# A gate product moved ahead of a head's q and k in the filling work of a decoder block on one Trainium2 core

## The chip, the core and the metric

The kernel runs on one core of one Trainium2 chip. The metric is the device time of one execution in microseconds. The engines are TensorE (PE, with its weight loads as PEld), VectorE (DVE), ScalarE (ACT), GpSimd (POOL) and SyncE (SP, which issues the loads). PSUM is the memory that PE writes its products to.

## The reference

One layer of a decoder block for 512 tokens of width 1024: an input projection, two causal attention branches (MLA with 8 heads, differential attention with 4 heads), a gated merge, an output projection and a SwiGLU network of width 2816.

```python
xn = rmsnorm(x, norm_mix_g[l])
proj = jnp.einsum('bsd,de->bse', xn, w_in[l])
q_lat, kv_lat, k_rope, dq, dk, dv, gate_pre = jnp.split(proj, split_idx, axis=-1)
...
o_mla = causal_attention(q_mla, k_mla, v_mla).reshape(B, S, MLA_WIDTH)
...
o1 = causal_attention(dq[..., 0, :], dk[..., 0, :], dv)
o2 = causal_attention(dq[..., 1, :], dk[..., 1, :], dv)
o_diff = rmsnorm(o1 - lam * o2, diff_subln_g[l]) * (1.0 - lambda_init)
...
gates = jax.nn.sigmoid(gate_pre + b_gate[l])
g_mla, g_diff = gates[..., :D_MODEL], gates[..., D_MODEL:]
merged = (g_mla * jnp.einsum('bse,ed->bsd', o_mla, w_branch_mla[l])
          + g_diff * jnp.einsum('bse,ed->bsd', o_diff, w_branch_diff[l]))
x = x + jnp.einsum('bsd,de->bse', merged, w_out[l])
hn = rmsnorm(x, norm_ffn_g[l])
hid = jax.nn.silu(jnp.einsum('bsd,df->bsf', hn, w_ffn_gate[l])) * jnp.einsum('bsd,df->bsf', hn, w_ffn_up[l])
x = x + jnp.einsum('bsf,fd->bsd', hid, w_ffn_down[l])
```

## The kernel before

Every product of full precision is made of three matmuls (`mm3`, L299 to L301): operands are split into a rounded high part and the remainder, and high times high, high times low and low times high are added up in PSUM. Weights come in tiles of 128 x 1024 (`weights`): SP loads them into `raw` (four buffers), ACT rounds them (L261) and DVE takes the difference (L266) into `w` (three buffers).

The attention of a head is a chain. Four blocks of scores (L627) of 128, 256, 384 and 512 columns go through a maximum on DVE (L631), an exponential on ACT (L159), a reciprocal (L634) and scaling (L681 and L680 for a differential head); PE transposes them (L653), ACT and DVE split the transposes into `PT` (L246, L250), and PE multiplies with V (L664, or L774 in MLA). For a differential head a norm follows in `diff_norm`: PE sums the squares with two matmuls against `ones_r` (L699) and ACT takes a logarithm and an exponential (L159).

This chain leaves PE idle, so it is filled with products that the attention doesn't wait for at once. Tables of "filling items" say which product is written into which stage: `FILL_MLA` for four pairs of MLA heads, `FILL_DIFF` for four differential heads. `("qk", h)` makes q and k of head h (two products of 24 matmuls, each read by the rotary on DVE with a shuffle, L558, and a multiplication, L559, and finished on POOL, L560 and L561). `("v", c)` makes V of heads 2c and 2c + 1: two PSUM tiles of 48 matmuls of 256 columns, scaled into SBUF by ACT (L248) and DVE (L252). `("gate", b, m)` makes one tile of gate pre-activations (24 matmuls), read by one DVE multiplication (L481). A scheduler orders all instructions on each engine ahead of time; attention has the higher priority (`urgent`), filling items take what is left, in the order in which they are written. Each engine then works its list in that order.

All these products write PSUM tiles called `ps_mm`, of which there are three buffers, taken in turn: a product starts only when the product three before it has been read.

Behind the last head, ACT loads another table and makes 16 sigmoids in place (`sigmoids`, L488), held behind the last exponential. The 16 products of the branches (`branch`, 12 matmuls each, also in `ps_mm`) are each multiplied with a gate by DVE (L792), which needs the sigmoid. The first of them need only the MLA result and begin while the last head's norm is still under way. The output projection and the SwiGLU network follow.

Of the kernel before, what the change touches and what calls it, by code (L numbers as in the profile page):

```python
# [47 lines left out]
            [("mqk", 2), ("mr", 2), ("gate", 0, 3), ("gate", 0, 4), ("mv", 1)],  # L48
            [("mqk", 3), ("mr", 3), ("qk", 0)],
            [("qk", 1)]]  # L50
FILL_DIFF = [[("qk", 2), ("v", 1)],
             [("qk", 3), ("gate", 0, 5), ("gate", 0, 6)],
             [("gate", 0, 7), ("gate", 1, 0), ("gate", 1, 1)],
             [("gate", 1, m) for m in range(2, KD)]]
PBUFS = dict(mm=3, sc=2, tr=2, pv=1)
# [33 lines left out]
def build(ctx, nc, tc, a, out):  # L89
# [51 lines left out]
    def urgent():  # L141
        return attention
# [351 lines left out]
    def fill(work):  # L494
        for kind, *args in work:
            if kind == "gate":
                gate(*args)
            elif kind == "v":
                diff_v(*args)
            elif kind == "qk":  # L500
                qk[args[0]] = diff_qk(*args)
            elif kind == "pe":
                pe[args[0]] = mla_pe(*args)
            elif kind == "mv":
                mv[args[0]] = mla_v(*args)
            elif kind == "mqk":
                mqk[args[0]] = mla_qk(*args)
            elif kind == "mr":
                mla_rope(args[0], mqk[args[0]], pe[args[0] // 2])
# [301 lines left out]
    for h in range(4):  # L811
        parts_first[0] = True
        fill(FILL_DIFF[h])
        with urgent():
# [185 lines left out]
```

## Time and profile before

| | |
|---|---|
| median of 3 runs | 740.13 us (740.10 to 741.04) |
| profiled execution | 740.23 us, span 738.5 us |
| busy PE, DVE, ACT, POOL | 729.0, 413.6, 333.7, 48.4 us |
| MLA attention ends, differential attention goes on | about 180 us |
| last differential head's PV products end, branch products start | 276 us, 280 us |

Busy time is how long an engine had an instruction under way; matmuls overlap, so their pace is read from one start to the next. Timeline rows give the start, the duration, engine, line, operation, output and inputs, shape and number of merged instructions, and in brackets the idle time before and who ended it.

### The profile page before, as it was taken

Reading aid. Unit: us, or ns where it says so; the run is one execution under the profiler, and the core shown is the slowest. Engines: PE = TensorE matmul, PEld = TensorE weight load, DVE = VectorE, ACT = ScalarE, POOL = GpSimd, SP = SyncE. Lnnn points to the kernel's source line nnn. Section 1 sums busy time; section 2 is a strip of 40 time slices with the busy share of each in tenths; the row PEclk is TensorE's granted clock in tenths of the full one; section 3 lists DMA queues with packets and bytes.
Section 4 is the critical chain, followed back from the end, with each engine's and each line's share of the span. In section 5 each row is a group of like instructions: output and inputs, shape, how many; then the busy total and the mean of one; then the engine's idle time right before and its main releaser. Section 6 shows DMA issues by size and latency. Waiting matters only on the chain.

```text
span 738.5 us, 9543 instructions
## 1 busy us (share of the span) xinstructions
PE 729.0 (99%) x3602; PEld 617.2 (84%) x3602; DVE 413.6 (56%) x812; ACT 333.7 (45%) x613; POOL 48.4 (7%) x45
## 2 busy tenths in 40 slices
PE   9999999999999999999999999999999999999996
PEld 7978988888888888888898888888888888888885
DVE  7789789988898765793634333333233232222514
ACT  7765678676766526561433223223232231212314
POOL 1000000322041101000000000000000000000303
PEclk9999999999999999999999999999999999999999
DMA  9615455323433312346204233332333323223203
GB/s 335 196 59 138 120 129 137 93 59 85 115 86 86 114 59 87 114 161 210 84 3 143 86 108 92 90 110 86 105 94 88 112 86 102 98 88 113 86 1 114
DMA packets 100414, 78.82 MB, mean 107 GB/s; under 512 B 6416, under 2 KB 87056, under 8 KB 100368
## 3 DMA queue, kind: packets, MB, share of 16 engines
q1 hardware_dynamic: 100080, 78.13, 35.9%
q8 instruction: 28, 0.46, 0.3%
q14 instruction: 18, 0.15, 0.1%
q10 hardware_dynamic: 288, 0.08, 0.0%
HBM read 71.91 MB, written 2.10 MB: 100 GB/s over the span
## 4 chain that ended last, share of the span: by engine, by line
PE 96%; DVE 3%; ACT 0%; issue 0%; DVEq 0%
PE ps_mm L299 25%; PE ps_mm L300 25%; PE ps_mm L301 25%; PE ps_sc L627 3%; PE ps_tr L653 2%; PE ps_tr L301 2%; PE ps_sc L300 2%; PE ps_sc L299 2%; PE ps_sc L301 2%; PE ps_tr L299 2%; PE ps_tr L300 2%; PE ps_pv L774 1%; PE ps_pv L664 1%; PE ps_pv L301 1%; PE ps_pv L300 1%; PE ps_pv L299 1%
## 5 line engine op out<-in xcount | busy, mean ns | idle before, releaser
L261 ACT ACTIVATE w<-raw 128x1024 fp32r<-128x1024 f32 (+3 forms) x110 | 109.4, 998 | 253.5 <-issue 150.7
L266 DVE TENSOR_TENSOR w<-raw,w 128x1024 fp32r<-128x1024 f32 (+3 forms) x114 | 133.7, 1175 | 159.8 <-ACT w L261 159.5
L299 PE MATMUL ps_mm<-X,w 128*128 128x512 f32 (+1 forms) x568 | 217.3, 383 | 0.1
L300 PE MATMUL ps_mm<-X,w 128*128 128x512 f32 (+1 forms) x568 | 216.8, 382 | 0.0
L301 PE MATMUL ps_mm<-X,w 128*128 128x512 f32 (+1 forms) x568 | 216.4, 381 | 0.0
L299 PEld LDWEIGHTS ps_mm<-X,w 128*128 128x128 f32 x568 | 106.7, 188 | 20.4 <-issue 0.3
L300 PEld LDWEIGHTS ps_mm<-X,w 128*128 128x128 f32 x568 | 106.9, 188 | 20.0 <-issue 0.2
L301 PEld LDWEIGHTS ps_mm<-X,w 128*128 128x128 f32 x568 | 106.8, 188 | 20.0
L905 DVE TENSOR_TENSOR t<-t,ps_mm 128x512 f32<-128x512 f32 x22 | 15.1, 688 | 66.8 <-PE ps_mm L301 66.1
L159 ACT ACTIVATE P<-P,sm 128x128 f32<-128x128 f32 (+3 forms) x64 | 35.7, 558 | 21.4 <-DVE sm L631 21.0
L931 POOL TENSOR_TENSOR L<-L,P 128x512 f32<-128x512 f32 (+1 forms) x9 | 12.6, 1421 | 434.8 <-ACT t L930 434.8
L627 PE MATMUL ps_sc<-L,L 96*128 96x128 f32 (+7 forms) x160 | 37.3, 327 | 0.2 <-DVE sm L631 0.2
L300 PE MATMUL ps_mm<-w,L 128*128 128x512 f32 (+1 forms) x100 | 37.3, 373 | 0.0
L299 PE MATMUL ps_mm<-w,L 128*128 128x512 f32 (+1 forms) x100 | 37.1, 373 | 0.0
L301 PE MATMUL ps_mm<-w,L 128*128 128x512 f32 (+1 forms) x100 | 37.0, 373 | 0.0
L300 PE MATMUL ps_mm<-L,w 128*128 128x512 f32 x90 | 35.4, 394 | 0.0
L299 PE MATMUL ps_mm<-L,w 128*128 128x512 f32 x90 | 35.4, 395 | 0.0
L301 PE MATMUL ps_mm<-L,w 128*128 128x512 f32 x90 | 35.1, 390 | 0.0
L631 DVE CUSTOM_DVE_ANT_0 P<-ps_sc,mask 128x128 f32<-128x128 f32 (+3 forms) x64 | 30.5, 477 | 5.8 <-PE ps_sc L627 5.0
L246 ACT ACTIVATE L<-t 64x512 fp32r<-64x512 f32 (+2 forms) x47 | 29.2, 621 | 6.9 <-PE ps_pv L301 3.7
L627 PEld LDWEIGHTS ps_sc<-L,L 96*128 96x128 f32 (+1 forms) x160 | 26.7, 189 | 3.3 <-DVE sm L631 0.4
L250 DVE TENSOR_TENSOR L<-t,L 128x512 fp32r<-128x512 f32 (+2 forms) x37 | 26.3, 711 | 3.5 <-ACT L L246 3.1
(271 smaller groups left out, 1136.8 us busy)
## 6 DMA issues: line engine op xcount, KB each, us to landing
raw<-w_in SPq DMA_DIRECT2D x28, 512.0 KB, 4.0
raw<-w_ffn_gate SPq DMA_DIRECT2D x22, 512.0 KB, 3.9
raw<-w_ffn_up SPq DMA_DIRECT2D x22, 512.0 KB, 3.9
raw<-w_ffn_down SPq DMA_DIRECT2D x22, 512.0 KB, 3.6
L<-x SPq DMA_DIRECT2D x8, 512.0 KB, 7.3
L<-L SPq DMA_DIRECT2D x32, 128.0 KB, 3.7
raw<-w_out SPq DMA_DIRECT2D x8, 512.0 KB, 3.9
L<-xt SPq DMA_DIRECT2D x8, 256.0 KB, 4.4
```

The costliest lines, as they stand in the source:

```text
L159: return nc.scalar.activation(**kw)
L246: nc.scalar.activation(out=hi, in_=src, func=AF.Copy, scale=scale)
L250: nc.vector.tensor_sub(out=lo, in0=src, in1=r32(hi))
L261: nc.scalar.activation(out=o, in_=i, func=AF.Copy)
L266: (nc.vector if w_eng[1] == 'dve' else nc.gpsimd).tensor_sub(out=o, in0=i, in1=r32(hi))
L299: nc.tensor.matmul(out=o, lhsT=lh, rhs=rh, start=start, stop=False)
L300: nc.tensor.matmul(out=o, lhsT=lh, rhs=rl, start=False, stop=False)
L301: return nc.tensor.matmul(out=o, lhsT=ll, rhs=rh, start=False, stop=stop)
L627: nc.tensor.matmul(out=ps[:, :n], lhsT=q[:, i * P:n], rhs=k[:, 0:n], start=j == 0, stop=j == last)
L631: nc.vector.tensor_tensor_reduce(out=m, in0=ps[:, :n], in1=mask[:, S - n:], scale=-1.0, scalar=3.4e38, op0=ALU.add, op1=ALU.min, accum_out ...
L653: nc.tensor.transpose(out=ps[:, c:c + P], in_=blocks[i][:, j * P:(j + 1) * P], identity=ident)
L905: nc.vector.tensor_mul(out=g, in0=g, in1=ps)
```

## The change

Gate product 5 of the first branch is written one stage earlier, ahead of q and k of the third differential head. The number of instructions of each kind stays the same.

```diff
-FILL_DIFF = [[("qk", 2), ("v", 1)],
-             [("qk", 3), ("gate", 0, 5), ("gate", 0, 6)],
+FILL_DIFF = [[("gate", 0, 5), ("qk", 2), ("v", 1)],
+             [("qk", 3), ("gate", 0, 6)],
```

The scheduler's lists differ from there to the first branch products. PE's list on V, near the end of the MLA attention, before: `ps_sc_2303` and `ps_sc_2304` are the fourth score block of differential head 0, `ps_mm_2179` is the second tile of V.

```order
L627 MATMUL ps_sc_2304<-L_1567,L_1566 128x512
L774 MATMUL ps_pv_2014<-PT_1994,L_1320 128x256
L774 MATMUL ps_pv_2014<-PT_1994,L_1320 128x128
L774 MATMUL ps_pv_2014<-PT_1994,L_1304 128x512
L774 MATMUL ps_pv_2014<-PT_1994,L_1304 128x384
L774 MATMUL ps_pv_2014<-PT_1994,L_1320 128x256
L774 MATMUL ps_pv_2014<-PT_1994,L_1320 128x128
L653 MATMUL ps_tr_2332<-ident,P_2233 128x128
L627 MATMUL ps_sc_2529<-L_1817,L_1815 128x128
L627 MATMUL ps_sc_2529<-L_1817,L_1816 128x128
L299 MATMUL ps_mm_2179<-w_2117,X_61 128x256
```

The same place after, from the fourth score block on: `ps_sc_2334` and `ps_sc_2335` are its two maps, `ps_mm_2156` the first tile of V.

```order
L627 MATMUL ps_sc_2334<-L_1567,L_1565 128x512
L627 MATMUL ps_sc_2334<-L_1567,L_1566 128x512
L301 MATMUL ps_mm_2156<-w_2153,X_62 128x256
L299 MATMUL ps_mm_2156<-w_2153,X_62 128x256
L300 MATMUL ps_mm_2156<-w_2153,X_62 128x256
L301 MATMUL ps_mm_2156<-w_2153,X_62 128x256
L627 MATMUL ps_sc_2335<-L_1567,L_1565 128x512
L627 MATMUL ps_sc_2335<-L_1567,L_1566 128x512
L653 MATMUL ps_tr_2356<-ident,P_2264 128x128
L774 MATMUL ps_pv_2014<-PT_1994,L_1320 128x256
```

Before, the first tile of V was done ahead of the fourth score block; now its last four matmuls stand between the two maps. Behind these rows come the other five PV matmuls, a transpose, two scores, two transposes and then V's second tile (`ps_mm_2210`).

DVE's list at the same place, before: `ps_mm_2033` is q of the third head.

```order
L634 RECIPROCAL sm_2294<-sm_2293 128x1
L631 ISA P_2301,sm_2309<-ps_sc_2303,mask 128x512
L631 ISA sm_2309 128x1
L679 TENSOR_TENSOR sm_2294<-sm_2294,neg_lam 128x1
L558 STREAM_SHUFFLE t_2059<-ps_mm_2033 128x512
L559 TENSOR_TENSOR t_2058<-ps_mm_2033,tab_595 128x512
```

And after, where q is `ps_mm_2064`:

```order
L631 ISA P_2332,sm_2340<-ps_sc_2334,mask 128x512
L631 ISA sm_2340 128x1
L681 SCALAR_TENSOR_TENSOR P_2309<-P_2309,sm_2319,P_2310 128x384
L634 RECIPROCAL sm_2342<-sm_2341 128x1
L558 STREAM_SHUFFLE t_2090<-ps_mm_2064 128x512
L559 TENSOR_TENSOR t_2089<-ps_mm_2064,tab_595 128x512
```

The reciprocal of this same score block (`sm_2341` is the sum that its exponential on ACT makes) now stands ahead of the rotary's reads of q.

PE's list behind the last differential head, before: `ps_tr_3229` is that head's norm, `ps_mm_3264` and `ps_mm_3278` are the first two branch products, and `ps_mm_3297` and `ps_mm_3311` the third and fourth.

```order
L299 MATMUL ps_mm_3278<-L_829,w_3261 128x512
L300 MATMUL ps_mm_3278<-L_829,w_3261 128x512
L699 MATMUL ps_tr_3229<-L_3226,ones_r 128x512
L301 MATMUL ps_mm_3278<-L_829,w_3261 128x512
L299 MATMUL ps_mm_3278<-L_1179,w_3261 128x512
```

After:

```order
L299 MATMUL ps_mm_3297<-L_1778,w_3294 128x512
L699 MATMUL ps_tr_3229<-L_3226,ones_r 128x512
L300 MATMUL ps_mm_3297<-L_1778,w_3294 128x512
L301 MATMUL ps_mm_3297<-L_1778,w_3294 128x512
L299 MATMUL ps_mm_3311<-L_829,w_3294 128x512
```

The second norm matmul stood three matmuls into the second branch product, with 22 of the second and third behind it; now it stands two matmuls ahead of the fourth one. The last head's PV products end 19 matmuls later in PE's list than before, the branch products follow directly, and the norm comes in among them.

## The prediction

> **What bounds the kernel now.** I read the busy times first, then who TensorE waits for, then its timeline at those places. The first two rows are from the page, the next three are all the waits of TensorE (PE) behind the first two microseconds (total, times, longest).
>
> ```profile
> span 738.5 us, 9543 instructions
> PE 729.0 (99%) x3602; PEld 617.2 (84%) x3602; DVE 413.6 (56%) x812; ACT 333.7 (45%) x613; POOL 48.4 (7%) x45
> ...
> PE ps_mm L299 <- DVE t L559: 0.9, 1, 0.9
> PE ps_pv L664 <- ACT PT L246: 0.2, 1, 0.2
> PE ps_sc L627 <- DVE sm L631: 0.2, 1, 0.2
> ```
>
> PE works 729.0 of 738.5 us. The change adds and removes no matmul, so the sum is about PE's waits alone. Two places hold all the waits shown. The first is the end of the MLA attention, where the second half of V starts (column two is the time of a row, matmuls overlap, so I count from start to start):
>
> ```profile
> 176.58 0.63 PE L627 MATMUL ps_sc<-L,L 128*128 128x512 f32 x2
> 177.05 0.57 PE L774 MATMUL ps_pv<-PT,L 128*128 128x512 f32 x2
> ...
> 178.53 1.08 PE L774 MATMUL ps_pv<-PT,L 128*128 128x256 f32 x6
> 179.45 0.28 PE L653 MATMUL ps_tr<-ident,P 128*128 128x128 f32 x1
> 179.91 0.44 PE L627 MATMUL ps_sc<-L,L 128*128 128x128 f32 x2 [0.18 <-DVE sm L631]
> 181.21 0.39 PE L299 MATMUL ps_mm<-w,X 128*128 128x256 f32 x1 [0.86 <-DVE t L559]
> 181.43 0.28 PE L300 MATMUL ps_mm<-w,X 128*128 128x256 f32 x1
> 181.55 0.28 PE L301 MATMUL ps_mm<-w,X 128*128 128x256 f32 x1
> ...
> 186.11 0.34 PE L627 MATMUL ps_sc<-L,L 128*128 128x128 f32 x2
> 186.29 0.33 PE L300 MATMUL ps_mm<-w,X 128*128 128x256 f32 x1
> ```
>
> A 256-wide matmul takes 0.12 us from start to start (181.43 to 181.55), two small scores 0.18 (186.11 to 186.29), a transpose about 0.11. Unhindered, the matmul at 181.43 would start at 179.45 + 0.11 + 0.18 + 0.12 = 179.86. Place A loses 1.57 us. The wait ends with the rotary reads (L558, L559) that free q's PSUM buffer. The second place, at the first PV product of differential head 0:
>
> ```profile
> 193.73 0.51 PE L627 MATMUL ps_sc<-L,L 128*128 128x384 f32 x2
> 194.46 0.82 PE L664 MATMUL ps_pv<-PT,L 128*128 128x512 f32 x2 [0.22 <-ACT PT L246]
> 195.33 0.50 PE L299 MATMUL ps_mm<-X,w 128*128 128x512 f32 x1
> 195.67 0.40 PE L300 MATMUL ps_mm<-X,w 128*128 128x512 f32 x1
> ...
> 199.32 0.51 PE L627 MATMUL ps_sc<-L,L 128*128 128x384 f32 x2
> 199.66 0.39 PE L301 MATMUL ps_mm<-X,w 128*128 128x512 f32 x1
> ```
>
> Two 384-wide scores take 0.34 (199.32 to 199.66), a 512-wide matmul 0.23 and a 384-wide one 0.17, so 195.67 would be 193.73 + 0.34 + 0.40 + 0.23 = 194.70. Place B loses 0.97 us. No more than 2.54 us can be won in this stretch.
>
> **The change, place A.** The gate's 24 matmuls go ahead of q's and leave stage 1: on PE zero. Its load and two weight splits move one slot earlier on SP, ACT and DVE, and those of q, k and V one slot later; the second V load slides behind the first head's two copies on SP. I give that nothing: q's and k's 48 matmuls, 11 us, still stand ahead of V's first one. What counts is the ring of three `mm` buffers. V's first half now takes the gate's buffer, which one L481 frees, in place of a buffer of the MLA stage. V's second half still takes q's buffer, so the wait for L559 stays; what changes is the work of both engines ahead of it. Before, DVE did the maximum of the fourth score block (L631) and then L558 and L559, but it came to them late:
>
> ```profile
> 179.18 0.67 DVE L631 CUSTOM_DVE_ANT_0 P<-ps_sc,mask 128x512 f32<-128x512 f32 x1
> 180.48 0.68 DVE L559 TENSOR_TENSOR t<-ps_mm,tab 128x512 f32<-128x512 f32 x1
> ```
>
> The scores had ended at 176.58 + 0.63 = 177.21, and DVE was 1.97 us behind. Now more V matmuls lie between the score blocks and DVE is on time, but the order puts L681 and a reciprocal (L634) ahead of L558, and the reciprocal waits for ACT's exponential. The same row of four stands later in the trace:
>
> ```profile
> 204.06 0.68 DVE L631 CUSTOM_DVE_ANT_0 P<-ps_sc,mask 128x512 f32<-128x512 f32 x1
> 204.66 0.61 DVE L681 SCALAR_TENSOR_TENSOR P<-P,sm,P 128x384 f32<-128x384 f32 x1
> 205.63 0.17 DVE L634 RECIPROCAL sm<-sm 128x1 f32<-128x1 f32 x1 [0.35 <-ACT P L159]
> ...
> 206.94 0.68 DVE L559 TENSOR_TENSOR t<-ps_mm,tab 128x512 f32<-128x512 f32 x1
> ```
>
> From L631 to L634 is 1.57 us, then 0.08, 0.64 for the shuffle (206.31 to 206.94 there) and 0.68: 2.97. Counted from the start T of the first score matmul, the scores end at T + 0.63, so q's buffer is free at T + 3.6. PE, by the new order, has until V's second half: scores 0.47, four 256-wide 0.48, scores 0.47, a transpose 0.11, six PV 0.92 (178.53 to 179.45), a transpose 0.11, scores 0.18, two transposes 0.22: T + 2.96. It waits 0.64, and 0.15 for starting again (181.21 to 181.43 is 0.22 where 0.12 is usual, and 0.05 to the start). So A costs 0.8 instead of 1.57: **-0.8 us**. Bounds: gone (-1.57) and unchanged (0).
>
> **Place B.** There are now 13 instead of 6 filling matmuls between the last transposes and the first PV product, which would cover the wait for `PT`. But k's product after it still takes the buffer of V's first half, read last by a DVE instruction, and DVE comes to that late for a reason that stays:
>
> ```profile
> 183.57 1.69 DVE L681 SCALAR_TENSOR_TENSOR P<-P,sm,P 128x384 f32<-128x384 f32 x1
> 185.29 1.67 DVE L250 TENSOR_TENSOR L<-t,L 64x512 fp32r<-64x512 f32 x1
> ...
> 183.24 3.18 POOL L561 TENSOR_TENSOR t<-t,t 128x512 f32<-128x512 f32 x2
> ```
>
> L681 of that width took 0.61 at 204.66; beside POOL's L561 it took 1.69. Nothing in the change moves POOL away from DVE. Bounds: -0.97 (gone) and +1.1 (one more such hold falls ahead of the buffer's last reader). I take **0**, the row of before.
>
> **Place C, the end of the last head.** Nobody waits there now. The rows show PE's two norm matmuls (the second at 283.59), ACT's chain from them, DVE's first gated product (L792) and the matmul that needs its buffer (288.81):
>
> ```profile
> 283.59 0.40 PE L699 MATMUL ps_tr<-L,ones_r 128*128 128x512 f32 x1
> 283.82 0.39 PE L301 MATMUL ps_mm<-L,w 128*128 128x512 f32 x1
> ...
> 288.81 0.39 PE L299 MATMUL ps_mm<-L,w 128*128 128x512 f32 x1
> ...
> 284.02 0.69 ACT L159 ACTIVATE t<-ps_tr,eps 128x512 f32<-128x512 f32 x1 [6.75 <-PE ps_tr L699]
> 284.74 0.63 ACT L159 ACTIVATE t<-t 128x512 f32<-128x512 f32 x1
> 285.39 1.28 ACT L488 ACT_TABLE_LOAD   x1
> 286.69 9.93 ACT L488 ACTIVATE L<-L,cols 128x512 f32<-128x512 f32 x16
> ...
> 287.44 0.69 DVE L792 TENSOR_TENSOR L<-L,ps_mm 128x512 f32<-128x512 f32 x1 [1.34 <-ACT L L488]
> ```
>
> From the second norm matmul to the end of L792 is 288.13 - 283.59 = 4.54 us: logarithm, exponential, table load, the first of 16 sigmoids, the product. Before, 22 branch matmuls stood between that norm matmul and the fourth branch product, 288.81 - 283.59 = 5.22 us; slack 0.68. Now only two stand there: the attention of the last head ends 19 matmuls later among the fillers, while the branch products start at once behind it. PE arrives 0.23 x 3 = 0.69 us after the norm matmul and waits 4.54 + 0.05 - 0.69 = 3.9 us, with 0.1 for the restart **+4.0 us**. Behind it PE was busy without a gap to the end, so nothing takes this back. Bounds: 3.8 and 4.1, since the whole chain is measured.
>
> **Sum.** -0.8 + 0 + 4.0 = +3.2 us. The profiled execution took 740.23 us; 743.4. The median of the three runs, 740.13, is 0.1 lower, less than I can resolve. Forecast 743.4 us, its own range 742.0 to 744.8.
>
> **A rule weighed.** PE's longest wait so far, 0.86 us, left the clock alone (0.12 us per 256-wide matmul right behind it). A wait of 3.9 us is not in this trace. The nearest row is the start:
>
> ```profile
> 1.19 4.45 PE L172 MATMUL ps_pv<-P 128*128 128x512 bf16 x10 [1.19 <-DVE P L168]
> 5.08 1.52 PE L299 MATMUL ps_mm<-L,X 128*128 128x384 f32 x3
> ```
>
> There ten 512-wide matmuls took 3.89 us, 0.39 each against 0.23 later. The Trainium skill, "TensorE: Matmul & The Clock Gate", Part 1, says that the array's clock falls to half after an idle window of about 3.4 us, which runs freely, and comes back after a busy one. The start's 0.39 goes its way without being the full half; no row here shows a wait of that length under load. By that rule the wait at C may or may not hold a whole window, and the sum would be 743.4 or the first rival's time.
>
> **Rivals.** First, the clock drops at C: PE is slow for up to the 5.4 us of the start (1.19 to 6.6), losing 1 - 0.23/0.39 = 0.41 of it, 2.2 us: 745.6. For it: the wait is four times the longest seen. Against: it must cover the time that makes the clock fall. Second, about no change: A and B both vanish because PE has one product more to hide them, and only C stays: -1.57 - 0.97 + 4.0 = +1.5, 741.7; a little less at C and it is inside 0.2%. For it: 13 instead of 6 matmuls at B. Against: the reciprocal at A and POOL at B. Third, faster: the fourth branch product doesn't wait for L792, because the buffer it takes isn't the one that I think; before, it started 0.68 us after L792 and so never showed the wait. Then A and B decide: -0.8 - 0.97 = -1.8, 738.4. It needs L792's end within about 1 us of PE's arrival, where the chain makes it 3.9. Against: three `mm` buffers in turn, and PE starting V's second half 0.05 us after L559 shows how closely such a buffer holds it.
>
> **How the numbers follow.** Forecast 0.70, clock 0.14, no change 0.11, faster 0.05. The measurement tells 0.2%, 1.5 us, from no change, that is 741.6 on the slow side. The second rival sits on that edge; half of it goes to the same and half to slower, and 0.03 of the forecast's lower end to the same. Slower 0.86, same 0.09, faster 0.05. The range takes in the second rival, from 741.4, and the first with 0.3 us to spare, to 745.9; left out are the faster rival and the outer parts of the other two.
>
> **What would show it.** In the waits of PE a new line for L299 behind DVE's L792 (or ACT's sigmoid) of about 3.9 us near 290; the L559 wait down to about 0.6; the wait at B between 0 and 2; the granted clock and the spacing right behind C. A fourth branch product that starts without a wait would make the forecast wrong, and so would a new wait between 200 and 285, where PE shows none now.

## The result, and the profile after

The changed kernel takes 745.43 us (median of 4 runs, 745.30 to 745.89), the kernel before beside it on the same chip 740.12: a ratio of 1.0069 with a 95% interval of 1.0057 to 1.0081. It is slower, as forecast, but 2.0 us above the forecast of 743.4 and outside the forecast's own range (742.0 to 744.8). It lies in the whole range (741.4 to 745.9) only because that takes in the first rival, the clock. The profiled execution took 745.30 us. Its first lines on the page, and all waits of TensorE behind the start (total, times, longest, us):

```profile
span 743.5 us, 9549 instructions
PE 730.3 (98%) x3602; PEld 617.9 (83%) x3602; DVE 411.7 (55%) x812; ACT 333.7 (45%) x613; POOL 48.3 (6%) x45
...
PE ps_mm L299 <- DVE L L792: 3.7, 1, 3.7
...
PE ps_mm L299 <- DVE t L559: 0.7, 1, 0.7
PE ps_mm L299 <- DVE L L252: 0.3, 1, 0.3
PE ps_tr L653 <- DVE PT L250: 0.2, 1, 0.2
```

As many matmuls as before, 1.3 us more of busy time, and a span that is 5.0 us longer. One wait is new and large: the fourth branch product for L792, place C. Its rows on TensorE, with the first gated product of DVE that frees its buffer:

```profile
287.60 0.40 PE L699 MATMUL ps_tr<-L,ones_r 128*128 128x512 f32 x1
287.83 0.39 PE L300 MATMUL ps_mm<-L,w 128*128 128x512 f32 x1
288.06 0.39 PE L301 MATMUL ps_mm<-L,w 128*128 128x512 f32 x1
292.19 0.80 PE L299 MATMUL ps_mm<-L,w 128*128 128x512 f32 x1 [3.74 <-DVE L L792]
292.78 0.63 PE L300 MATMUL ps_mm<-L,w 128*128 128x512 f32 x1
293.21 0.63 PE L301 MATMUL ps_mm<-L,w 128*128 128x512 f32 x1
...
295.67 0.39 PE L301 MATMUL ps_mm<-L,w 128*128 128x512 f32 x1
...
291.44 0.69 DVE L792 TENSOR_TENSOR L<-L,ps_mm 128x512 f32<-128x512 f32 x1 [1.34 <-ACT L L488]
```

From 288.06 the next matmul would have started at 288.29; it started at 292.19: 3.90 us. That is the forecast's 3.9. What follows was not in its sum: a matmul of this shape takes 0.23 us from start to start (287.83 to 288.06), and here 0.43 (292.78 to 293.21) until 295.3. From 292.19 to 295.67 eight matmuls took 3.48 us instead of 8 x 0.227 = 1.82: 1.66 us more, of which 0.1 is the usual restart. The table by stretches says why; column by column: stretch, its length, busy time and count of PE, PEld, DVE, ACT and POOL, granted clock of TensorE, DMA share, GB/s.

```profile
288.73:292.14 3.41, 0.00 (x0) 0.00 (x0) 1.39 (x3) 3.36 (x5) 1.26 (x1) 1.00 0.42 145
292.14:295.55 3.41, 3.36 (x8) 2.70 (x9) 2.39 (x4) 3.41 (x6) 0.00 (x0) 0.50 0.00 0
```

The stretches are cut where the trace's record of the clock has its steps. The granted clock is 0.50 from 292.14, just as TensorE gets its buffer, to 295.55, 3.41 us: the first rival. Behind it the matmuls are back at 0.23 (from 295.67 on). The 3.41 us ahead of the fall hold no work of TensorE at all.

### The profile page after: what moved, and what is told of

It reads as the page before. It is cut to its first block, busy times and chain, and to the rows that moved or that the text cites. A ratio compares the mean times of both kernels' runs of the same rounds, so it can differ in the third digit from the quotient of the medians.

```text
span 743.5 us, 9549 instructions
## 1 busy us (share of the span) xinstructions
PE 730.3 (98%) x3602; PEld 617.9 (83%) x3602; DVE 411.7 (55%) x812; ACT 333.7 (45%) x613; POOL 48.3 (6%) x45
## 4 chain that ended last, share of the span: by engine, by line
PE 95%; DVE 2%; ACT 2%; issue 0%; DMA 0%; DVEq 0%; ACTq 0%
PE ps_mm L300 25%; PE ps_mm L299 25%; PE ps_mm L301 25%; PE ps_sc L627 3%; PE ps_tr L653 2%; PE ps_sc L299 2%; PE ps_tr L301 2%; PE ps_sc L300 2%; PE ps_tr L299 2%; PE ps_tr L300 2%; PE ps_sc L301 2%; PE ps_pv L774 1%; PE ps_pv L664 1%; PE ps_pv L300 1%; PE ps_pv L301 1%; PE ps_pv L299 1%
## 5 line engine op out<-in xcount | busy, mean ns | idle before, releaser
L266 DVE TENSOR_TENSOR w<-raw,w 128x1024 fp32r<-128x1024 f32 (+3 forms) x114 | 133.3, 1172 | 158.6 <-ACT w L261 158.2
L299 PE MATMUL ps_mm<-X,w 128*128 128x512 f32 (+1 forms) x568 | 217.2, 383 | 0.3 <-DVE L L252 0.3
L299 PEld LDWEIGHTS ps_mm<-X,w 128*128 128x128 f32 x568 | 106.8, 188 | 21.0 <-DVE L L252 0.5
L299 PE MATMUL ps_mm<-L,w 128*128 128x512 f32 x90 | 36.3, 405 | 3.7 <-DVE L L792 3.7
L299 PE MATMUL ps_mm<-w,L 128*128 128x512 f32 (+1 forms) x100 | 37.2, 373 | 0.0
L300 PE MATMUL ps_mm<-L,w 128*128 128x512 f32 x90 | 36.1, 401 | 0.0
L301 PE MATMUL ps_mm<-L,w 128*128 128x512 f32 x90 | 35.6, 396 | 0.0
L250 DVE TENSOR_TENSOR L<-t,L 128x512 fp32r<-128x512 f32 (+2 forms) x37 | 26.4, 713 | 3.5 <-ACT L L246 3.1
```

The lines of the kernel that those rows point to most:

```text
L250: nc.vector.tensor_sub(out=lo, in0=src, in1=r32(hi))
L266: (nc.vector if w_eng[1] == 'dve' else nc.gpsimd).tensor_sub(out=o, in0=i, in1=r32(hi))
L299: nc.tensor.matmul(out=o, lhsT=lh, rhs=rh, start=start, stop=False)
L300: nc.tensor.matmul(out=o, lhsT=lh, rhs=rl, start=False, stop=False)
L301: return nc.tensor.matmul(out=o, lhsT=ll, rhs=rh, start=False, stop=stop)
```

## The experiments

**How long may the wait be before the clock falls?** Matmuls of 384 columns on constant data are put on TensorE ahead of the wait, in the changed kernel. They compute nothing that is used, and they don't move the end of L792, so the time differs only by the clock. Their number was 12, 4 and 8 (the loop's bound):

```diff
-                mm3(ps, [w[s][:, k, i * P:(i + 1) * P] for s in range(2)], [o[k][:, s, :] for s in range(2)],
+                last = mm3(ps, [w[s][:, k, i * P:(i + 1) * P] for s in range(2)], [o[k][:, s, :] for s in range(2)],
...
+            if (b, m, i) == (0, 2, 0):
+                idle = PS("pv")
+                with tc.issue_after(last.ins):
+                    for _ in range(12):
+                        nc.tensor.matmul(out=idle[:, :384], lhsT=mask[:, :P], rhs=mask[:, :384], start=True, stop=True)
```

With 12:

> The changed kernel with twelve matmuls of 384 columns on constant data (their result is not read) on TensorE behind the third branch product, so that it works through about 1.9 us of the 3.74 us wait at place C. Theory: the wait for L792 itself costs 3.9 us and stays, but the clock no longer falls, so the slow matmuls behind it (0.43 us from start to start) go back to 0.23: 745.4 - 1.7 = 743.7 us. Rival, that the slow start belongs to any wait for a buffer: 745.4. Rival, that the added matmuls come on top: 747.3.

Measured 743.85 us (743.69 to 744.68), ratio to the kernel before 1.0046 (1.0033 to 1.006). The rows of TensorE at the wait (L792 is L797 in this kernel) and the stretch behind:

```profile
288.20 2.12 PE L795 MATMUL ps_pv<-mask 128*128 128x384 bf16 x12
292.10 0.50 PE L299 MATMUL ps_mm<-L,w 128*128 128x512 f32 x1 [1.77 <-DVE L L797]
292.43 0.39 PE L300 MATMUL ps_mm<-L,w 128*128 128x512 f32 x1
292.66 0.40 PE L301 MATMUL ps_mm<-L,w 128*128 128x512 f32 x1
...
292.00:294.00 2.00, 1.90 (x8) 1.61 (x9) 2.00 (x5) 2.00 (x4) 0.00 (x0) 1.00 0.00 0
```

The fourth branch product starts at the same time as in the changed kernel (292.10 against 292.19), but its matmuls then follow each other by 0.23 us, the clock at 1.00. 745.43 - 743.85 = 1.6 us is the clock's whole part, by the time as by the rows.

With 4:

> The same with four such matmuls, which leaves about 3.1 us of idle time, less than the 3.41 us between the clock's steps in the trace. If only a window without any work lets the clock fall: 743.7 us and no fall. If a window that is mostly idle is enough (at the end of the profiled run it fell after a window with 0.86 us of work in it): 745.4 in the runs in which the windows fall so, a granted clock of 0.5 for 3.4 us behind place C.

Measured 745.40 us, ratio 1.0061 (1.0048 to 1.0074). The wait is 3.1 us; here the clock fell after TensorE had already started again:

```profile
288.42 0.82 PE L795 MATMUL ps_pv<-mask 128*128 128x384 bf16 x4
292.31 0.50 PE L299 MATMUL ps_mm<-L,w 128*128 128x512 f32 x1 [3.07 <-DVE L L797]
...
292.88 0.40 PE L301 MATMUL ps_mm<-L,w 128*128 128x512 f32 x1
293.11 0.55 PE L299 MATMUL ps_mm<-L,w 128*128 128x512 f32 x1
293.47 0.63 PE L300 MATMUL ps_mm<-L,w 128*128 128x512 f32 x1
...
289.78:293.19 3.41, 0.88 (x4) 0.75 (x5) 2.07 (x4) 3.40 (x5) 1.26 (x1) 1.00 0.18 62
293.19:296.60 3.41, 3.41 (x10) 2.64 (x9) 1.47 (x3) 3.41 (x7) 0.00 (x0) 0.50 0.00 0
```

Three matmuls run at full pace and the fourth is slowed half-way, at 293.19, where the clock's record has its step. In the 3.41 us up to there TensorE was at work for 0.88 us, 26%. So a window that is idle for the most part is enough. One of the five runs had no fall, by its time and mean clock (744.09 us, 0.997 where the others have 0.995), as windows that run freely would make it; no trace was taken of it.

With 8:

> The changed kernel with 8 matmuls of 384 columns on constant data behind the third branch product, between the 4 and the 12 already run. TensorE's wait for L792 is then 3.74 - 8 x 0.17 = 2.4 us, and the end of L792 doesn't move, so the time differs only by the clock: 743.7 if it stays up, 745.4 if it falls. With 12 (wait 1.8) it never fell, with 4 (wait 3.1) it fell in 4 of 5. A window of the clock record is 3.41 us; one that holds the whole wait has at least 28% work. If the bound lies between the 26% that fell and the 46% that didn't, some of the runs may fall, by how the windows happen to lie; if it is close to 26%, none: 743.7.

Measured 745.28 us, ratio 1.0065 (1.0053 to 1.0078): 743.7 does not happen. The wait is 2.4 us:

```profile
PE ps_mm L299 <- DVE L L797: 2.4, 1, 2.4
...
PE ps_sc L627 <- DMA L<-L: 0.6, 1, 0.6
```

The profiled run had a mean clock of 0.998 and took 744.54 us, with a wait for a load of 0.6 us that is elsewhere in the kernel; without that, 743.9 and no fall. The other four took 745.09 to 745.43 at 0.995. A window of 3.41 us that holds all of this wait is busy for at least 1 - 2.42 / 3.41 = 29%. The 46% of the expectation is a window at the end of the kernel before, 730.12 to 733.54 us, in which TensorE stopped at 731.68 and behind which the clock stayed up for one window more. So the bound, if it is a share of work, lies between 29% and 46%, not close to 26%, and that none would fall was wrong. For those four runs only their mean clock and time show the fall; no trace was taken of them. In the profiled run, windows of 3.413 us counted from the clock's rise at 5.41 us meet at 292.13 and cut the wait in two; the one up to there was busy for 1.84 us, 54%, which agrees with a clock that stayed up.

**Does the lost cover alone make the wait?** The kernel before, with the gate product where it was, but with the last head's two norm matmuls held behind the fifth and the tenth matmul of the third branch product (the branch's matmuls are written out so that they can be named, and the first three products and their weights are written ahead of the norm):

```diff
-            nc.tensor.matmul(out=ps, lhsT=ones_r, rhs=sqs[s], start=s == 0, stop=s == 1)
+            with tc.issue_after(pins[s].ins) if pins else nullcontext():
+                nc.tensor.matmul(out=ps, lhsT=ones_r, rhs=sqs[s], start=s == 0, stop=s == 1)
...
+    third = ahead[0, 2, 0][1]
...
+        o_diff.append(diff_norm(*parts[3], pins=(third[4], third[9])))
```

> The kernel before, with the last head's two norm matmuls pinned behind the fifth and the tenth matmul of the third branch product, where the changed kernel has them; the gate stays where it was. Theory: place C alone makes the loss, 3.9 us of wait and 1.7 us of slow clock: 740.1 + 5.6 = 745.7 us, places A and B as before (2.5 us lost), the first 1400 matmuls in the old order. Rival, that the gate's move itself costs through A and B or through weights that come late: 740.1 us.

Measured 746.29 us (745.74 to 747.95), ratio 1.008 (1.0066 to 1.0094). The wait of place A from its list of waits, the rows of TensorE at C (L299 is L790 in the branch, L792 is L804) and two stretches, cut at the steps of the clock:

```profile
PE ps_mm L299 <- DVE t L559: 0.9, 1, 0.9
...
293.50 0.80 PE L790 MATMUL ps_mm<-L,w 128*128 128x512 f32 x1 [3.74 <-DVE L L804]
294.09 0.63 PE L791 MATMUL ps_mm<-L,w 128*128 128x512 f32 x1
...
292.77:296.18 3.41, 2.68 (x6) 2.17 (x7) 3.08 (x5) 3.41 (x6) 0.00 (x0) 0.50 0.00 0
296.18:299.60 3.42, 3.42 (x9) 2.67 (x8) 0.50 (x1) 3.42 (x7) 0.00 (x0) 0.50 0.00 0
```

The wait is the changed kernel's to the hundredth, 3.74 us, and the wait for L559 at place A stands as before. So the norm's place ahead of the fourth branch product is sufficient for C, whatever stands in the first differential stage. In this run the clock stayed low for two windows instead of one. It is the longest of the four (747.95 us): besides the second slow window it holds a wait of 0.6 us for a load, elsewhere in the kernel. Two of the others took 745.74 and 745.85 us, where 745.7 was expected, and one 746.72.

**Take the dependence away.** In the changed kernel the branch products take five PSUM buffers in turn instead of three, so the fourth needs no read of the first; the two of `ps_sc`, which the attention has left, serve as well:

```diff
+    ring = [0]
...
-            ps = PS("mm")
+            ps = PS(("mm", "mm", "mm", "sc", "sc")[ring[0] % 5])
+            ring[0] += 1
```

> The changed kernel with the branch products in five PSUM buffers, mm and the two score buffers in turn (the attention is over by then), so that the fourth product needs no buffer that waits for a sigmoid and two more products cover 5.4 us. Theory: the wait at C and the fall of the clock go, A and B stay: 745.4 - 5.7 = 739.7 us, about the kernel before. Rival, that the first sigmoid or the weights hold the products anyway: 743 to 745.

Measured 739.72 us (739.56 to 740.46), ratio 0.9991 (0.9982 to 1.0). All waits behind the start:

```profile
span 737.9 us, 9548 instructions
...
PE ps_mm L299 <- DVE t L559: 0.7, 1, 0.7
PE ps_mm L299 <- DVE L L252: 0.3, 1, 0.3
PE ps_tr L653 <- DVE PT L250: 0.2, 1, 0.2
```

The wait at C is gone with the clock's fall: 743.5 - 737.9 = 5.6 us of span. A and B stay as in the changed kernel. The same edit in the kernel before is the control:

> The kernel before, with the five buffers alone. Nobody waits at C there (the buffer is free 0.68 us before it is taken), so the theory says no change: 740.1, waits of TensorE as before (0.9 for L559, 0.2, 0.2). If five buffers are worth something by themselves, as a rival for the gain of 5.7 us that they brought to the changed kernel: 739 or less.

Measured 740.25 us, ratio 0.9999 (0.999 to 1.0008): five buffers are worth nothing where nobody waits. This leaves the value of the gate's move without C, the difference of the two: 739.72 - 740.25 = -0.5 us, and the spans, 737.9 and 738.4, say the same. It is small against the spread of either kernel's runs (0.9 and 0.8 us).

**Is V taking q's buffer the cause at A and B?** V is written ahead of q and k in the table of the kernel before, the gate product is left in place, and the branch has five buffers:

```diff
-FILL_DIFF = [[("qk", 2), ("v", 1)],
+FILL_DIFF = [[("v", 1), ("qk", 2)],
```

> The kernel before with V written ahead of q and k of the third differential head, the gate product left where it was, and the branch products in five PSUM buffers instead of three. If the wait at place A comes from V's second tile taking q's buffer, it goes here, since V takes buffers that were read long before: -1.57 us. If place B is only the buffer of V's first tile, it goes too: -0.97. With five buffers the branch products don't wait at C. Theory: 740.1 - 2.5 = 737.6, up to 738.3 if one hold of DVE by POOL stays. Rival (the wait at A is DVE's lateness and finds another buffer): L559 or L252 stays in the waits of TensorE with 0.7 to 1 us, and 739.5 to 740.1.

Measured 737.64 us (737.38 to 738.43), ratio 0.9965 (0.9953 to 0.9977). Beside the start, one wait of TensorE is left:

```profile
span 736.5 us, 9537 instructions
...
PE ps_sc L627 <- DMA L<-L: 0.7, 1, 0.7
```

No wait at A or B, and 2.6 us less than with the same five buffers in the old order (740.25), where the prediction had found 2.54 us to be won. It is the fastest version here. The edit changes the order of several engines at once, so it shows what the order is worth, and not what each of the two buffers costs. DVE was still slow beside POOL there: L250 took 1.68 us at 190.42 us, and TensorE waited for nothing of it. That such a slow stretch costs TensorE something only where a product needs a buffer that DVE reads behind it is inferred from these two orders, not tested. With three buffers:

> The same order, V ahead of q and k, with the three buffers of the kernel before. The last head's second norm matmul stands 18 matmuls ahead of the fourth branch product here, 18 x 0.23 = 4.1 us, and the chain from it to the end of L792 takes 4.54: a wait of 0.5 to 1 us for L792, too short for the clock to fall. 738.2 to 739.0, that is 0.5 to 1 us above the same order with five buffers. If moving filling work ahead costs 4 us at C wherever it is moved from: 741 or more.

Measured 738.90 us (738.70 to 739.99), ratio 0.9982 (0.9974 to 0.9991), 1.3 us above five buffers. TensorE's wait there and the pace behind it:

```profile
281.99 0.40 PE L699 MATMUL ps_tr<-L,ones_r 128*128 128x512 f32 x1
...
287.28 0.50 PE L299 MATMUL ps_mm<-L,w 128*128 128x512 f32 x1 [1.04 <-DVE L L792]
287.62 0.39 PE L300 MATMUL ps_mm<-L,w 128*128 128x512 f32 x1
287.85 0.40 PE L301 MATMUL ps_mm<-L,w 128*128 128x512 f32 x1
...
284.76 1.86 DVE L266 TENSOR_TENSOR w<-raw,w 128x1024 fp32r<-128x1024 f32 x1
286.55 0.68 DVE L792 TENSOR_TENSOR L<-L,ps_mm 128x512 f32<-128x512 f32 x1
```

The wait for L792 is 1.04 us and the clock stays up (0.23 us from start to start). It is at the upper end of what was expected, because a weight split (L266) stood ahead of L792 on DVE: from the norm matmul to the end of the wait it is 287.28 - 281.99 = 5.29 us here and 292.19 - 287.60 = 4.59 in the changed kernel, 0.7 more. With that told, the cost at C follows the number of matmuls between the norm and the fourth branch product: 22 of them and no wait, 17 and 1.04 us, 2 and 3.74 us.

## Why the prediction was right in sign and short by 2 us

**Place A: right.** -0.8 was forecast. Rows after: TensorE, the reciprocal on DVE, and DVE's read that ends the wait:

```profile
183.36 0.63 PE L627 MATMUL ps_sc<-L,L 128*128 128x512 f32 x2
...
186.12 0.39 PE L299 MATMUL ps_mm<-w,X 128*128 128x256 f32 x1 [0.65 <-DVE t L559]
186.34 0.28 PE L300 MATMUL ps_mm<-w,X 128*128 128x256 f32 x1
...
184.66 0.17 DVE L634 RECIPROCAL sm<-sm 128x1 f32<-128x1 f32 x1 [0.35 <-ACT P L159]
...
185.38 0.68 DVE L559 TENSOR_TENSOR t<-ps_mm,tab 128x512 f32<-128x512 f32 x1
```

Counted as in the prediction, the matmul at 186.34 would have started at 183.36 + 0.47 + 0.11 + 0.92 + 0.11 + 0.18 + 0.22 + 0.12 = 185.49. A costs 0.85 us; it was 1.57. The wait of 0.65 was forecast as 0.64. The reciprocal, with its wait for ACT, takes 0.35 + 0.09 = 0.44 us of DVE's time ahead of q's reads, and L681 ahead of it 0.61; without these two the reads would have ended before TensorE was ready. No run took them away.

**Place B: inside its bounds, but 0.4 us more than forecast, and the reason given doesn't explain it.** The forecast took the row of before because DVE would be as slow beside POOL as before. It was less so: before, L681 and L250 took 1.69 and 1.67 us instead of 0.61 and 0.68, together 2.1 us more; after, of these two only L250 was slow, 1.1 us more. Still DVE's reads of V's buffers end late:

```profile
189.47 1.76 DVE L250 TENSOR_TENSOR L<-t,L 64x512 fp32r<-64x512 f32 x1
...
200.57 0.86 DVE L252 SCALAR_TENSOR_TENSOR L<-ps_mm,sm,L 128x256 fp32r<-128x256 f32 x2
...
198.43 0.51 PE L627 MATMUL ps_sc<-L,L 128*128 128x384 f32 x2
198.77 0.57 PE L664 MATMUL ps_pv<-PT,L 128*128 128x512 f32 x2
199.38 0.62 PE L627 MATMUL ps_sc<-L,L 128*128 128x384 f32 x2
200.24 0.55 PE L653 MATMUL ps_tr<-ident,P 128*128 128x128 f32 x3 [0.25 <-DVE PT L250]
201.10 0.50 PE L299 MATMUL ps_mm<-X,w 128*128 128x512 f32 x1 [0.31 <-DVE L L252]
201.43 0.40 PE L300 MATMUL ps_mm<-X,w 128*128 128x512 f32 x1
```

Two scores 0.34, two PV products 0.40, two scores 0.34, three transposes 0.33 and a matmul 0.23 make 1.64; from 198.43 to 201.43 it took 3.00. B costs 1.36 instead of 0.97. The 13 filling matmuls did cover the first wait for `PT` (the PV product at 198.77 follows the scores by 0.34, as if unhindered), but the transposes now wait for DVE as well, and k's product still waits for a read of V. DVE's rows show no wait from 188.78 to 201.4 us, so its backlog as a whole makes these reads late; which part of it makes B larger stays open. 0 was forecast and +0.4 measured, inside the bounds of -0.97 and +1.1. The two waits at 200.24 and 201.10 fall where the prediction said that a new wait would make it wrong (200 to 285), but they belong to place B, which comes later in this kernel.

**Place C: the wait right, its consequence not.** The wait and its restart were forecast at 4.0 and measured at 3.90 + 0.10. The term that failed is the one that the sum left out of the likeliest case: the clock, +1.56 us (1.66 less the restart). With it the sum is -0.7 + 0.4 + 4.0 + 1.6 = +5.3, where the span grew by 5.0. Compared matmul by matmul, the 1,561st starts 0.54 us earlier than before (286.91 against 287.45) and the 1,621st 5.07 later (306.12 against 301.05): C as a whole costs 5.6, and what lies ahead of it brings 0.54, of which A and B account for 0.3. The other 0.2 us lie in small steps that I don't resolve.

**The rivals.** The first rival, the clock, had 0.14 and is what happened, by their mean clock of 0.995 to 0.996 in all four runs of the changed kernel. That its price of 745.6 us lies so near is in part luck: the clock cost 0.6 us less than it says, and B, put at nothing, 0.4 more. What failed is the argument against it: the wait would have to "cover the time that makes the clock fall". The Trainium skill, "TensorE: Matmul & The Clock Gate", Part 1, gives an idle window of about 3.4 us that runs freely. Under a strict reading, that every instant of the window be idle, a wait of 3.74 us holds such a window only by luck of its place, in 0.33 of 3.41 us or about one position in ten, and it would have fallen rarely. The runs agree with the page on the length (slow stretches of 3.41 us), on the half clock (0.50) and on the free running (the clock first rises at 3.82 to 6.50 us in the ten traces, and in the changed kernel it falls 286.72 us later, 84 times 3.4133). They differ from that strict reading: the clock fell behind a window with 26% of work. With a bound of 29% to 46%, 3.74 us of idle time make the clock fall in about 68% of positions to all of them, an estimate from these figures; it fell in 4 of 4 runs, and by the mean clock of 0.993 to 0.995 in all 4 of the late norm. Knowing this, the rival deserves more chance than the forecast. Its price was somewhat high, 2.2 us for up to 5.4 slow ones, since the clock was back after one window of 3.41 us; measured 1.56 and 1.6. The second rival (A and B vanish) fell with the waits for L559 and L252 that stayed; they vanished where V went ahead of q and k. The third (no wait at C) fell at the row of 292.19.

## What to carry to other kernels

A filling item that is moved early can be paid for far behind: here the stage 100 us later lost the products that had covered a norm, an activation table and a sigmoid on the way to a PSUM buffer. Count, in the order, the matmuls between the head of such a chain and the product that needs its end, against the chain's length in the trace. A wait of TensorE of 2.4 us or more is to be priced with the slow matmuls behind it (here 1.6 us for each slow window of 3.41 us; waits of 1.8 us and less cost only themselves), and a further buffer can be a simpler remedy than a better order.

## What the hardware showed that was not expected

- The clock fell after windows that were idle only for the most part. Waits at C of 1.0 us (11 runs) and 1.8 us (5 runs) left it alone; in the runs with 2.4 us it fell in 4 of 5, with 3.1 us in 4 of 5, with 3.74 us in 4 of 4. One run of each has a trace, the others are told by their mean clock.
- The fall can come after the wait is over, 0.88 us in the kernel with 4 filling matmuls, and then slows matmuls that waited for nothing.
- It comes back after one window in the changed kernel (3.41 us, eight matmuls touched) but only after two in the kernel with the late norm. There the first slow window was busy for 2.68 of 3.41 us, 79%; in the changed kernel for 3.36, 98%. That the share of work decides this, too, fits both, but two windows don't show it.
